# V in 512 columns from four weight blocks held together, in place of two groups of 256

## The chip, the cores and the metric

The kernel runs on one core of one Trainium2 chip, written in Bass with the Tile layer. The metric is the time of one execution on the device in microseconds, as the median of several runs. The core has five engines that work in parallel and in order, each on its own queue: TensorE (PE; its weight loads are listed as PEld), VectorE (DVE), ScalarE (ACT), GpSimd (POOL) and SyncE (SP), which mainly issues DMA transfers. Matmul results go to PSUM, everything else lies in SBUF.

## The reference

One inference step of a streaming encoder layer: a mixer (attention over a band of keys beside a convolution), cross-attention to 256 memory tokens, and a SwiGLU feed-forward. There are 2048 prompt frames and 128 sample frames (8 streams of 16), so 17 tiles of 128 rows, of width 1024. What matters here is the mixer's input projection:

```
h = rmsnorm(x, g_mix_pre)
proj = h @ w_in                      # 1024 -> [q 512 | k 512 | v 512 | u_val 512 | u_gate 512]
q, k, v, u_val, u_gate = jnp.split(proj, ...)
att = band_attention(q, k_ext, v_ext, key_valid, rel_bias)   # 8 heads x 64
u = u_val * jax.nn.sigmoid(u_gate)   # then a depthwise convolution of width 31
```

The keys and values of the last 512 prompt frames and of the sample frames are outputs too.

## The kernel before

**Precision.** Each operand of a matmul is split into a high part (rounded to fp32r) and a low part, the remainder; `mm3` issues three matmuls per product, high by high (L290), high by low (L291) and low by high (L292). A weight block of 128 rows by 1024 words is loaded by SyncE's queue into one of three buffers `wf`, cast by ScalarE into a high buffer `wh` (L283), and the low part `wl` is the difference, by GpSimd in the projection (L285). There are four `wh` and four `wl`, given out in turn; a block can be split only when all matmuls that read the buffer's former block are done.

**The projection** (`phase_proj`) takes the 17 tiles in three groups of 6, 6 and 5 tiles, each in two halves of at most three tiles (384 columns). A group runs, in the order of the code: GLU (four pairs of weight blocks, 384-column matmuls; L605, L606 evict), the V stage, then q and k (eight blocks, `qk`). Transposes of the next group's normed rows (L337, evicted by L339 and L340) lie between. Beside this run the depthwise convolutions of the groups: for three of four channel blocks on VectorE (L523), for the fourth and for the sample rows on ScalarE (L532, the product) and GpSimd (L533, the sum); a call of `tick` draws some of these steps, at V as elsewhere. The product has two buffers, so ScalarE's L532 can be only two steps ahead of GpSimd.

**The V stage.** V is computed with the normed rows as weights and the V weights as the moving operand, so that a tile's rows lie in the partitions. It runs over two groups of 256 columns; for each, two weight blocks (512 input rows each) are loaded, and each tile gets 24 matmuls of 256 columns into the first half of a PSUM buffer. The buffers of 512 words are four (`mm`), given out in turn. ScalarE copies the result into the high half of `vv` (L656), VectorE writes the difference beside it (L657), and SyncE stores both to `vs` in DRAM (L658). `vv` has two buffers. For tiles 12 and later ScalarE also copies the plain values into `vo` (three buffers, L645), which go to the outputs.

**What sets the order.** The kernel is written once in program order; when it is built, a scheduler with a timeline of its own lays down each engine's order from dependences and priorities. Steps of the convolutions that `tick` draws are given a lower priority. So a change in one place can move instructions around it on all engines. `bias_tables` in the first group writes a table for the attention's bias through DRAM, a 2.5 MB transfer on GpSimd's DMA queue (`toep`, L267).

After the projection come the band attention (from about 611 us), the output projection, cross-attention and the feed-forward, the largest part.

Of the kernel before, what the change touches and what calls it, by code (L numbers as in the profile page):

```python
# [8 lines left out]
F32 = mybir.dt.float32  # L9
# [8 lines left out]
P = 128  # L18
D = 1024
KC = D // P  # L20
NPT = 16
S_TILE = 16
H = 8
DH = 64
# [116 lines left out]
class Build:  # L141
# [309 lines left out]
    def phase_proj(self):  # L451
        nc, A = self.nc, self.A
        pool, fa = self.ap, self.fa
        ps_mm = ps_tr = Region().lay(self.ps, 0, ("mm", 2, 4), ("tr", 2, 2), ("ca", 4, 1))
# [43 lines left out]
        def pump(q, n):  # L498
            while n > 0 and q:
                try:  # L500
                    with self.tc.high_priority(offset=-LOWP):
                        next(q[0])
                    n -= 1
                except StopIteration:
                    q.pop(0)
# [4 lines left out]
        def tick():  # L510
            for x, q in enumerate((vq, pq)):
                acc[x] = acc[x] + rates[gi][x] if q else 0.0
                n = int(acc[x])
                pump(q, n)
                acc[x] -= n
# [62 lines left out]
        for gi, subs in enumerate(GROUPS):  # L578
# [5 lines left out]
            hs = nxt  # L584
# [3 lines left out]
            for j in range(4):  # L588
# [6 lines left out]
                wv = self.wload(A["w_in"][12 + j])  # L595
                wg = self.wload(A["w_in"][16 + j])
                off = 0
                for hsub in hs:
                    _, _, n, npc = hsub
# [16 lines left out]
                src = lambda w, u=ut, n=L: u[:, w:w + n]  # L616
# [6 lines left out]
                if npr < len(tiles):  # L623
                    o = ct[:, L:L + P].rearrange("p (s w) -> p s w", w=DEC_S)
                    src = lambda w, j=j: us[:, j, :, w:w + DEC_S]
# [2 lines left out]
                self.bias_tables(Region().lay(fa, 0, ("fb", 3, 1), ("rv", 1, 1)), glu)  # L628
            prev_u = (uts, L)
            x_ = "x" if last else ""  # L630
            for cg in range(2):
                wv = [self.wload(A["w_v"][cg, kh]) for kh in range(2)]
                for hsub, sub in zip(hs, subs):
                    hh, hl, _, _ = hsub
                    for i, t in enumerate(sub):
                        ps = self.t(ps_mm, [P, 512], F32, "mm")
                        tc_ = slice(i * P, (i + 1) * P)
                        for k in range(KC):
                            wh, wl = wv[k // 4]
                            c = slice((k % 4) * 256, (k % 4 + 1) * 256)  # L640
                            self.mm3(ps[:, :256], hh[:, k, tc_], hl[:, k, tc_], wh[:, c], wl[:, c], k == 0, k == KC - 1)
                        tick()
                        if t >= 12:
                            vo = self.t(pool, [P, 256], F32, "vo")
                            nc.scalar.copy(vo[:, :], ps[:, :256])  # L645
                            if t == S_TILE:
                                nc.sync.dma_start(self.vsamp[:, cg * 256:(cg + 1) * 256], vo[:, :])
                                nc.sync.dma_start(
                                    A["new_att_v_new"][:, cg * 256:(cg + 1) * 256], vo[:, :])
                            else:  # L650
                                nc.sync.dma_start(
                                    A["new_att_v_prompt"][(t - 12) * P:(t - 11) * P, cg * 256:(cg + 1) * 256], vo[:, :])
                        if t != S_TILE:
                            vv = self.t(pool, [P, 4, P], F32R, "vv", 2)
                            src = ps[:, :256].rearrange("p (h d) -> p h d", d=DH)
                            nc.scalar.copy(vv[:, :, :DH], src)  # L656
                            nc.vector.tensor_tensor(vv[:, :, DH:], src, vv[:, :, :DH].bitcast(F32), ALU.subtract)  # L657
                            nc.sync.dma_start(self.vs[cg][:, :, t, :], vv[:, :, :].bitcast(F32))  # L658
# [967 lines left out]
def layout(inputs):  # L1626
    import numpy as np

    i = {k: np.asarray(v) for k, v in inputs.items()}
    c = np.ascontiguousarray  # L1630
    o = {}
    o["x_prompt"] = i["x_prompt"].reshape(2048, D)
    o["x_sample"] = i["x_sample"].reshape(P, D)
    o["mem_prompt"] = i["mem_prompt"].reshape(NM, D)
    o["cache_att_k"] = i["cache_att_k"].reshape(DEC_B, PAST, 512)
    o["cache_att_v"] = i["cache_att_v"].reshape(DEC_B, PAST, 512)
    o["cache_conv"] = i["cache_conv"].reshape(DEC_B * HALO, 512)
    o["cache_convT"] = i["cache_conv"].reshape(DEC_B, HALO, 4, P).transpose(3, 2, 0, 1).reshape(P, 4 * DEC_B, HALO)
    o["cache_att_kT"] = i["cache_att_k"].reshape(DEC_B, PAST, 4, P).transpose(0, 3, 2, 1)
    o["cache_mem_kT"] = (i["cache_mem_k"].reshape(DEC_B, NM, 2, 4, P).transpose(0, 2, 4, 3, 1)  # L1640
                         .reshape(DEC_B, 2, P, D))
    o["cache_mem_v"] = i["cache_mem_v"].reshape(DEC_B, NM, D)

    def colblocks(w):
        n = w.shape[1] // P
        return w.reshape(KC, P, n, P).transpose(2, 1, 0, 3).reshape(n, P, D)

    o["w_in"] = colblocks(i["w_in"][0])
    wv = i["w_in"][0][:, 1024:1536]
    o["w_v"] = wv.reshape(2, 4, P, 2, 256).transpose(3, 0, 2, 1, 4).reshape(2, 2, P, D)  # L1650
    o["w_out"] = i["w_out"].reshape(KC, P, D)
    o["w_mk"] = colblocks(i["w_mk"][0])
    o["w_mv"] = colblocks(i["w_mv"][0])
    o["w_mqT"] = i["w_mq"][0].T.reshape(KC, P, D)
    o["w_mq"] = i["w_mq"].reshape(KC, P, D)
    o["w_mo"] = i["w_mo"].reshape(KC, P, D)
    o["w_gate"] = colblocks(i["w_gate"][0])
    o["w_up"] = colblocks(i["w_up"][0])
    o["w_down"] = i["w_down"].reshape(NF, P, D)
    for n in ("g_mix_pre", "g_mix_post", "g_mem_pre", "g_mem_post", "g_mem_kv", "g_ffn_pre", "g_ffn_post"):  # L1660
        o[n] = i[n].reshape(D)
    o["conv_w"] = i["conv_w"][0].reshape(CW, 4, P).transpose(2, 1, 0)
    for n in ("conv_b", "cln_g", "cln_b"):
        o[n] = i[n].reshape(4, P).T
    o["rel_rev"] = i["rel_bias"][0][:, :0:-1]
    return {k: c(v) for k, v in o.items()}
# [38 lines left out]
```

## Time and profile before

| | |
|---|---|
| median of 3 runs | 2940.11 us (2939.65 to 2940.16) |
| the profiled execution | 2931.87 us, its span 2930.0 us, mean granted clock 0.996 |
| TensorE busy | 98% of the span |
| VectorE, ScalarE, GpSimd busy | 73%, 46%, 48% |
| V stages | 178.9 to 216, 358.5 to 393, 525.6 to 554 us |

A row of a timeline has the start in microseconds, the duration, the engine, the line of the kernel, the operation, the tiles (written <- read), the shape, and how many equal instructions it merges; in brackets stands how long the engine was idle before it and whose work ended that. A windows row has the stretch, its length, the busy time (and instructions) of PE, PEld, DVE, ACT and POOL, the granted TensorE clock as a share of full speed, the DMA engines' busy share and GB/s. Matmuls overlap, so their pace is read from start to start.

### The profile page before, as it was taken

The page shows a single profiled execution, that of the slowest core. Times are in us where ns is not written, and L with a number is a line of the kernel's source. Part 1 is how long each engine was busy: PE and PEld are TensorE (multiplying, and loading weights), DVE is VectorE, ACT ScalarE, POOL GpSimd, SP SyncE. Part 2 cuts the span into 40 slices and gives each one's busy share as a digit, 9 for nine tenths or more (in the row PEclk, how much of TensorE's full clock was granted, in tenths as well). Part 3 has the DMA queues.
Part 4 walks back from the last instruction along what each step waited for, and adds up shares of the span by engine and source line. Part 5 has one row for each costly group of instructions (what it writes and reads, how often), then busy time and mean ns, then how long its engine had stood idle before and what let it go on. Part 6 is the DMA issues. An engine that isn't in the chain of part 4 may idle for free.

```text
span 2930.0 us, 45557 instructions
## 1 busy us (share of the span) xinstructions
PE 2878.5 (98%) x16688; PEld 2641.6 (90%) x16688; DVE 2131.4 (73%) x3082; ACT 1339.1 (46%) x2631; POOL 1416.2 (48%) x1334
## 2 busy tenths in 40 slices
PE   9999999989999999999999999999999999999998
PEld 8999999988978887888879999999999999888786
DVE  7687895989985666344559788788888998655656
ACT  4435465678873444232344333433344444333433
POOL 1268495831123443254557555465556775424413
PEclk9999999999999999999999999999999999999999
DMA  8645253665635664233364333544334436756664
GB/s 290 246 135 192 88 164 111 221 225 179 228 132 172 221 223 151 67 127 103 129 199 175 116 134 116 200 156 152 143 137 161 143 143 220 233 171 226 226 217 147
DMA packets 201458, 499.53 MB, mean 170 GB/s; under 512 B 19801, under 2 KB 91361, under 8 KB 192394
## 3 DMA queue, kind: packets, MB, share of 16 engines
q1 hardware_dynamic: 186306, 427.01, 43.2%
q0 software_dynamic: 14928, 69.61, 6.4%
q8 instruction: 131, 2.15, 0.3%
q14 instruction: 93, 0.76, 0.1%
HBM read 365.45 MB, written 141.81 MB: 173 GB/s over the span
## 4 chain that ended last, share of the span: by engine, by line
PE 44%; DVE 3%; DMA 2%; POOL 1%; issue 1%; ACT 0%; SPq 0%; DVEq 0%; POOLq 0%; ACTq 0%
PE psb L292 14%; PE psb L291 14%; PE psb L290 14%; PE psb L298 1%; DMA sbf<-x 1%; PE psb L1373 1%; DMA sbf<-hn 0%; DVE sbr L1588 0%; DMA sbf<-in_w_gate_dram 0%; DVE sbr L1396 0%; DVE sbx L1396 0%; POOL sbf L348 0%; DMA hn<-sbf 0%; DVE flexb L1458 0%; DVE flexb L1460 0%
## 5 line engine op out<-in xcount | busy, mean ns | idle before, releaser
L290 PE MATMUL psb<-sbr 128*128 128x384 f32 (+3 forms) x2808 | 940.3, 336 | 3.9 <-DVE sbx L657 1.5
L291 PE MATMUL psb<-sbr 128*128 128x384 f32 (+3 forms) x2356 | 804.1, 341 | 0.5 <-DVE sbr L340 0.3
L292 PE MATMUL psb<-sbr 128*128 128x512 f32 (+3 forms) x1848 | 633.9, 345 | 4.0 <-DVE sbr L1588 4.0
L290 PEld LDWEIGHTS psb<-sbr 128*128 128x128 f32 x2808 | 529.8, 189 | 33.1 <-DVE sbx L657 1.9
L292 PE MATMUL psb<-sbr,sbx 128*128 128x384 f32 (+2 forms) x1484 | 475.3, 321 | 0.0
L291 PEld LDWEIGHTS psb<-sbr 128*128 128x128 f32 x2356 | 444.2, 189 | 27.6 <-DVE sbr L340 1.0
L292 PEld LDWEIGHTS psb<-sbr 128*128 128x128 f32 x1848 | 348.4, 189 | 33.8 <-DVE sbr L1588 6.8
L298 PE MATMUL psb<-sbr 128*128 128x512 f32 x1200 | 292.7, 393 | 2.4 <-ACT sbr L1266 1.1
L1396 DVE TENSOR_TENSOR sbr<-sbf,sbr 128x512 fp32r<-128x512 f32 x258 | 262.2, 1019 | 39.7 <-ACT sbr L1395 38.5
L1395 ACT CAST sbr<-sbf 128x512 fp32r<-128x512 f32 x258 | 159.2, 620 | 277.9 <-PE psb L291 231.9
L292 PEld LDWEIGHTS psb<-sbr,sbx 128*128 128x128 f32 x1484 | 279.7, 189 | 0.1
L523 DVE SCALAR_TENSOR_TENSOR psb<-sbf,psb 128x768 f32<-128x768 f32 (+1 forms) x290 | 264.3, 912 | 6.2
L298 PEld LDWEIGHTS psb<-sbr 128*128 128x128 f32 x1200 | 222.0, 189 | 48.3 <-POOL sbr L1231 1.3
L1588 DVE TENSOR_TENSOR sbr<-sbf,sbr 128x384 fp32r<-128x384 f32 (+2 forms) x242 | 168.7, 720 | 96.4 <-ACT sbr L1587 95.4
L285 POOL TENSOR_TENSOR sbx<-sbf,sbr 128x1024 fp32r<-128x1024 f32 (+1 forms) x62 | 153.7, 2481 | 80.3 <-ACT sbr L283 69.2
L1587 ACT CAST sbr<-sbf 128x384 fp32r<-128x384 f32 (+2 forms) x242 | 112.6, 483 | 174.4 <-PE psb L291 162.3
L1518 POOL TENSOR_TENSOR sbf<-sbf 128x512 f32<-128x512 f32 x77 | 107.6, 1401 | 165.0 <-DMA sbf<-in_w_down_dram 163.4
L533 POOL TENSOR_TENSOR flexb<-flexb,flexb 128x128 f32<-128x128 f32 (+1 forms) x180 | 168.6, 937 | 26.2 <-ACT flexb L532 17.1
L290 PE MATMUL psb<-sbr,sbx 128*128 128x384 f32 (+1 forms) x524 | 170.6, 327 | 1.3 <-ACT sbr L1375 0.7
L1395 ACT CAST sbx<-sbf 128x512 fp32r<-128x512 f32 x153 | 94.7, 620 | 162.1 <-PE psb L291 149.3
L1396 DVE TENSOR_TENSOR sbx<-sbf,sbx 128x512 fp32r<-128x512 f32 x153 | 154.4, 1011 | 15.1 <-ACT sbx L1395 14.8
L1390 POOL TENSOR_TENSOR sbf<-sbf 128x512 f32<-128x512 f32 x66 | 97.8, 1481 | 108.0 <-DVE sbr L1396 50.8
(330 smaller groups left out, 6084.9 us busy)
## 6 DMA issues: line engine op xcount, KB each, us to landing
af<-flexb SPq DMA_DIRECT2D x33, 1344.0 KB, 5.9
sbf<-in_w_down_dram SPq DMA_DIRECT2D x154, 256.0 KB, 3.6
sbf<-in_w_gate_dram SPq DMA_DIRECT2D x66, 512.0 KB, 3.3
sbf<-in_w_up_dram SPq DMA_DIRECT2D x66, 512.0 KB, 3.4
sbf<-af SPq DMA_DIRECT2D x85, 384.0 KB, 4.1
sbf<-x SPq DMA_DIRECT2D x49, 512.0 KB, 3.7
sbf<-in_w_in_dram SPq DMA_DIRECT2D x48, 512.0 KB, 3.9
sbr<-ks POOLq DMA_DIRECT2D x16, 1024.0 KB, 8.5
```

The costliest lines, as they stand in the source:

```text
L285: self.lo_engine.tensor_tensor(lo[:, c], wf[:, c], hi[:, c].bitcast(F32), ALU.subtract)
L290: nc.tensor.matmul(ps, lh, rh, start=start, stop=False, **kw)
L291: nc.tensor.matmul(ps, lh, rl, start=False, stop=False, **kw)
L292: nc.tensor.matmul(ps, ll, rh, start=False, stop=stop, **kw)
L298: nc.tensor.matmul(y[o], l, r[:, o * 512:(o + 1) * 512], start=start and x == 0, stop=stop and x == 2)
L523: nc.vector.scalar_tensor_tensor(acc if w < CW - 1 else o, src(w), cwt[:, j, w:w + 1], acc, ALU.mult, ALU.add)
L533: nc.gpsimd.tensor_tensor(o, o, v, ALU.add)
L1395: nc.scalar.copy(hs[j][:, :], src[j])
L1396: nc.vector.tensor_tensor(ls[j][:, :], src[j], hs[j][:, :].bitcast(F32), ALU.subtract)
L1518: nc.gpsimd.tensor_tensor(acc[:, :], acc[:, :], q[:, :], ALU.add if s > 0 else ALU.subtract)
L1587: nc.scalar.copy(ch[:, m], a[:, x, m])
L1588: nc.vector.tensor_tensor(cl[:, m], a[:, x, m], ch[:, m].bitcast(F32), ALU.subtract)
```

## The change

The V stage holds four weight blocks of 256 input rows by 512 columns, and runs once over the tiles. A tile gets 24 matmuls of 512 columns into a whole PSUM buffer; the block changes every six matmuls. The two halves of the result are then copied, subtracted and stored one after the other with the same instructions as before, and `tick` is called twice per tile. The layout of the V weights in DRAM follows.

```
-            for cg in range(2):
-                wv = [self.wload(A["w_v"][cg, kh]) for kh in range(2)]
-                for hsub, sub in zip(hs, subs):
...
-                        for k in range(KC):
-                            wh, wl = wv[k // 4]
-                            c = slice((k % 4) * 256, (k % 4 + 1) * 256)
-                            self.mm3(ps[:, :256], hh[:, k, tc_], hl[:, k, tc_], wh[:, c], wl[:, c], k == 0, k == KC - 1)
-                        tick()
...
+            wv = [self.wload(A["w_v"][kq]) for kq in range(4)]
+            for hsub, sub in zip(hs, subs):
+                hh, hl, _, _ = hsub
+                for i, t in enumerate(sub):
+                    ps = self.t(ps_mm, [P, 512], F32, "mm")
+                    tc_ = slice(i * P, (i + 1) * P)
+                    for k in range(KC):
+                        wh, wl = wv[k // 2]
+                        c = slice((k % 2) * 512, (k % 2 + 1) * 512)
+                        self.mm3(ps[:, :], hh[:, k, tc_], hl[:, k, tc_], wh[:, c], wl[:, c], k == 0, k == KC - 1)
+                    tick()
+                    tick()
+                    for cg in range(2) if t >= 12 else ():
+                        cc = slice(cg * 256, (cg + 1) * 256)
+                        vo = self.t(pool, [P, 256], F32, "vo")
+                        nc.scalar.copy(vo[:, :], ps[:, cc])
...
+                    if t != S_TILE:
+                        for cg in range(2):
                             vv = self.t(pool, [P, 4, P], F32R, "vv", 2)
-                            src = ps[:, :256].rearrange("p (h d) -> p h d", d=DH)
+                            src = ps[:, cg * 256:(cg + 1) * 256].rearrange("p (h d) -> p h d", d=DH)
                             nc.scalar.copy(vv[:, :, :DH], src)
                             nc.vector.tensor_tensor(vv[:, :, DH:], src, vv[:, :, :DH].bitcast(F32), ALU.subtract)
                             nc.sync.dma_start(self.vs[cg][:, :, t, :], vv[:, :, :].bitcast(F32))
...
-    o["w_v"] = wv.reshape(2, 4, P, 2, 256).transpose(3, 0, 2, 1, 4).reshape(2, 2, P, D)
+    o["w_v"] = wv.reshape(4, 2, P, 512).transpose(0, 2, 1, 3).reshape(4, P, D)
```

In the changed kernel the plain copies stand in line 646; L656, L657 and L658 keep their numbers.

More of the change, by code (lines that the diff above doesn't have):

```diff
@@ L630, in phase_proj @@
             x_ = "x" if last else ""
-            for cg in range(2):
-                wv = [self.wload(A["w_v"][cg, kh]) for kh in range(2)]
-                for hsub, sub in zip(hs, subs):
[L634 to L637, printed above, removed]
-                        for k in range(KC):
-                            wh, wl = wv[k // 4]
-                            c = slice((k % 4) * 256, (k % 4 + 1) * 256)
-                            self.mm3(ps[:, :256], hh[:, k, tc_], hl[:, k, tc_], wh[:, c], wl[:, c], k == 0, k == KC - 1)
-                        tick()
[L643 to L653, printed above, removed]
@@ new lines, in phase_proj @@
+            wv = [self.wload(A["w_v"][kq]) for kq in range(4)]
[14 more added lines that the diff above has]
+                        nc.scalar.copy(vo[:, :], ps[:, cc])
+                        if t == S_TILE:
+                            nc.sync.dma_start(self.vsamp[:, cc], vo[:, :])
+                            nc.sync.dma_start(A["new_att_v_new"][:, cc], vo[:, :])
+                        else:
+                            nc.sync.dma_start(A["new_att_v_prompt"][(t - 12) * P:(t - 11) * P, cc], vo[:, :])
+                    if t != S_TILE:
+                        for cg in range(2):
```

## Prediction

> **What bounds the kernel now.** I read the page's busy times first, then the windows view over the stage that the change touches (179 to 554 us, in three parts), then TensorE's timeline for its pace and its gaps, then the timelines of ScalarE and GpSimd for what feeds it.
>
> ```profile
> span 2930.0 us, 45557 instructions
> PE 2878.5 (98%) x16688; PEld 2641.6 (90%) x16688; DVE 2131.4 (73%) x3082; ACT 1339.1 (46%) x2631; POOL 1416.2 (48%) x1334
> ```
>
> TensorE is busy for 98% of the span. Windows of the three V stages and of the entry to the attention (columns: window; its length; busy time and instructions of PE, PEld, DVE, ACT, POOL; granted clock; DMA share; GB/s):
>
> ```profile
> 179.00:199.00 20.00, 20.00 (x169) 20.00 (x168) 16.71 (x20) 9.94 (x13) 17.67 (x10) 1.00 0.56 190
> 199.00:216.00 17.00, 15.51 (x128) 15.07 (x127) 12.90 (x18) 8.61 (x16) 11.75 (x7) 1.00 0.61 197
> 358.00:393.00 35.00, 35.00 (x293) 35.00 (x292) 31.37 (x40) 21.07 (x30) 31.57 (x18) 1.00 0.45 137
> 525.00:554.00 29.00, 29.00 (x244) 29.00 (x243) 26.39 (x40) 20.93 (x54) 23.18 (x34) 1.00 0.72 226
> 610.00:640.00 30.00, 22.46 (x125) 17.80 (x124) 22.24 (x60) 22.27 (x59) 8.15 (x16) 0.83 0.54 195
> ```
>
> In the V stages TensorE leaves 1.5 us idle in the first and nothing in the others. So whatever the change takes from TensorE's work there is won in full, and whatever wait it puts before TensorE is lost in full.
>
> **The matmuls.** The change turns 816 matmuls of 256 columns (17 tiles x 2 column groups x 8 x 3) into 408 of 512. TensorE's timeline gives both paces, start to start:
>
> ```profile
> 178.93 0.28 PE L290 MATMUL psb<-sbr 128*128 128x256 f32 x1
> ...
> 358.45 0.28 PE L290 MATMUL psb<-sbr 128*128 128x256 f32 x1
> ...
> 392.87 0.28 PE L292 MATMUL psb<-sbr 128*128 128x256 f32 x1
> ...
> 554.37 0.34 PE L290 MATMUL psb<-sbr 128*128 128x384 f32 x1
> ...
> 2599.69 0.39 PE L290 MATMUL psb<-sbr 128*128 128x512 f32 x1
> ...
> 2605.81 0.39 PE L290 MATMUL psb<-sbr 128*128 128x512 f32 x1
> ```
>
> The second and third are the 1st and 288th matmul of the second V stage: 34.42/287 = 0.120 us. The last two are 27 steps apart in the last phase: 6.12/27 = 0.2267 us. The first row begins the first V stage; the one at 554.37 follows the third, which thus began 240 x 0.120 earlier, at 525.6. Two of 256 cost 0.240, one of 512 costs 0.227; the difference of 0.0132 us, 408 times, is **-5.4 us** (-1.9, -1.9, -1.6 by stage). The stages shrink to 144 x 0.2267 = 32.6, 32.6 and, with five tiles, 27.2 us. The Trainium skill (TensorE: Matmul & The Clock Gate, in the part on 56 against 53.3 ns) puts the fixed cost of a warm matmul at about 2.5 ns beyond its columns; by that 408 matmuls fewer would save only 1.0 us and the sum below would be 4.4 us higher. Here the rows show some 13 ns of it, and I go by the rows.
>
> The two gaps of the first stage come from V copies that were late to free a PSUM buffer:
>
> ```profile
> 200.46 0.39 PE L290 MATMUL psb<-sbr 128*128 128x256 f32 x1 [0.78 <-DVE sbx L657]
> 204.30 0.39 PE L290 MATMUL psb<-sbr 128*128 128x256 f32 x1 [0.70 <-DVE sbx L657]
> ```
>
> A V tile now fills one whole buffer in place of two halves, so four buffers hold 21.8 us of V work and not 11.5; these waits go: **-1.5 us**. What is late next in that place is below.
>
> **The start of a stage.** Weights are split by ScalarE (L283) and then GpSimd (L285) into a ring of four high and four low buffers. A stage used four V blocks before and uses four now; only when each is needed changes. Before, the blocks of the second group were due 17 us in; now all four are due in the first tile.
>
> ```profile
> 179.00 1.05 ACT L283 CAST sbr<-sbf 128x1024 fp32r<-128x1024 f32 x1 [2.72 <-POOL sbx L285]
> ...
> 180.13 2.58 POOL L285 TENSOR_TENSOR sbx<-sbf,sbr 128x1024 fp32r<-128x1024 f32 x1 [1.76 <-ACT sbr L283]
> ```
>
> This is the last V block of the first stage, ready at 182.7, 3.8 us after the stage began (178.9). The order of the built program covers it: TensorE runs the first two blocks' matmuls of tiles one and two (24 x 0.227 = 5.4 us) first, and in the third stage 44 matmuls. I cost the start at nothing; without that cover it would be 1 us a stage. By the same order the first tile ends with the stage's 46th matmul, 10.4 us in (third stage: 55th, 12.5 us).
>
> **The end of a stage.** This decides. The first K block that follows V takes the first buffer of the ring. Before, that was free halfway through V, and its split was long done:
>
> ```profile
> 375.61 2.42 POOL L285 TENSOR_TENSOR sbx<-sbf,sbr 128x1024 fp32r<-128x1024 f32 x1
> ```
>
> That is K's first block in the second stage, ready at 378.0, 15 us before V's last matmul. Now the buffer is held until six matmuls into the last V tile, 18 x 0.227 = 4.1 us before the end; cast and subtraction take 1.05 + 2.4 = 3.5 us. It would just do if ScalarE and GpSimd were at hand. But in ScalarE's order of the built program the cast stands behind the ninth of twelve V copies, and behind conv steps that wait for GpSimd (first stage):
>
> ```
> 113 L656 TensorCopy sbx<-psb 128x4x64 [waits DMAHW2,PE,Activation]
> 114 L532 Activation flexb<-sbf 128x768 [waits Pool]
> 115 L283 TensorCopy sbr<-sbf 128x1024 [waits PE]
> ```
>
> In GpSimd's, K's subtraction stands behind 14 conv adds of the stage. And a V copy needs one of two `vv` buffers, whose last store has to have landed. So the ninth copy comes no sooner than the first one plus four turns of that ring (copy, VectorE's subtraction, store). Before, it stood behind the third (at 195.36, below).
>
> *First stage.* Its stores share the DMA engines with a large table transfer:
>
> ```profile
> 184.94 1.32 POOL L267 DMA_DIRECT2D toep<-fd  x1 [0.24 <-issue]
> ...
> toep<-fd POOLq DMA_DIRECT2D x1, 2560.0 KB, 18.0
> ```
>
> ```profile
> 189.34 0.37 ACT L656 CAST sbx<-psb 128x256 fp32r<-128x256 f32 x1 [3.42 <-DMA vs<-sbx]
> ...
> 195.36 1.04 ACT L283 CAST sbr<-sbf 128x1024 fp32r<-128x1024 f32 x1
> ...
> 199.58 0.37 ACT L656 CAST sbx<-psb 128x256 fp32r<-128x256 f32 x1 [3.18 <-DMA vs<-sbx]
> 199.85 0.94 ACT L532 ACTIVATE flexb<-sbf 128x768 f32<-128x768 f32 x1
> ...
> 203.41 0.37 ACT L656 CAST sbx<-psb 128x256 fp32r<-128x256 f32 x1 [1.69 <-DMA vs<-sbx]
> ...
> 208.11 0.37 ACT L656 CAST sbx<-psb 128x256 fp32r<-128x256 f32 x1 [2.74 <-DMA vs<-sbx]
> ...
> 211.85 0.37 ACT L656 CAST sbx<-psb 128x256 fp32r<-128x256 f32 x1 [1.43 <-DMA vs<-sbx]
> ```
>
> ```profile
> 189.75 0.42 DVE L657 TENSOR_TENSOR sbx<-psb,sbx 128x256 fp32r<-128x256 f32 x1 [1.21 <-ACT sbx L656]
> ...
> 200.93 1.85 POOL L533 TENSOR_TENSOR flexb<-flexb,flexb 128x768 f32<-128x768 f32 x1 [0.25 <-ACT flexb L532]
> ```
>
> ```profile
> ACT sbx L656 <- DMA vs<-sbx: 14.4, 7, 3.4
> ```
>
> ```profile
> DMA to landing us min/median/max: 2.5/3.7/14.8
> ```
>
> (The last two fences: ScalarE's waits from 179 to 222 us, in sum, times, longest; and the V stores' time to landing, over all of them.) The table lands near 203, and the store for which the copy at 203.41 waited, that of the data subtracted at 189.75, took 13 us. The copies at 203.41, 208.11 and 211.85 are the fifth, seventh and ninth: turns of 4.7 and 3.7; I take 4.5, since the copy of a tile's second half now also waits for VectorE's subtraction of the first. After the change the first pair is copied at 189.5 and 191.5, its stores run in the same shadow, and the third copy comes at 201.5 to 203.3. Three turns on, the ninth is at 215.0 to 216.8. A conv step (0.9) and the cast (1.05) end at 217 to 219; GpSimd does its 14th add (1.85) after that conv step, then K's subtraction (2.4): ready at 220.4 to 222.2. TensorE ends V at 178.9 + 32.6 = 211.5, has 0.8 us of transposes and, by its order, 1.0 us of matmuls that need no low half. Stall: 7.1 to 8.9, I take **+8 us**. Bounds: 0 (stores land in 3 us; then the cast meets the 3.5 us that it has) and 12 (turns of 5.5).
>
> *Second stage.* No table. A turn is copy 0.37, subtraction 0.42 and the median 3.7 of a store, 4.5. First copy 10.7 us in, ninth at 28.7 (just after TensorE frees the buffer), cast 30.5; GpSimd's 14 adds of 1.85 and a gap or two also end near 30.5; low half 32.9. TensorE needs it at 32.6 + 0.8 + 1.0 = 34.4: **0**, covered by 1.5 us. A turn of 5.5 would use that up and cost 2.
>
> *Third stage.* Here K's cast stands behind the seventh copy, a prompt copy (L645, after L646) goes with each V copy, and VectorE reaches the first subtraction only after L558 and eleven conv steps (from 532.1, 0.74 each and a little between), near 541.
>
> ```profile
> 530.69 1.47 DVE L558 SCALAR_TENSOR_TENSOR flexb<-flexb 128x512 f32<-128x512 f32 x1
> 532.08 0.74 DVE L523 SCALAR_TENSOR_TENSOR psb<-sbf,psb 128x512 f32<-128x512 f32 x1
> ```
>
> ```profile
> 539.49 0.37 ACT L656 CAST sbx<-psb 128x256 fp32r<-128x256 f32 x1 [0.89 <-DMA vs<-sbx]
> 540.87 1.05 ACT L283 CAST sbr<-sbf 128x1024 fp32r<-128x1024 f32 x1
> ...
> 544.23 0.38 ACT L656 CAST sbx<-psb 128x256 fp32r<-128x256 f32 x1 [0.22 <-DMA vs<-sbx]
> ```
>
> Before, K's cast came at 540.87, 13 us ahead of need, and a turn was 544.23 - 539.49 = 4.7. After: first copy 538.5, its store from 541 lands near 545; third copy 545, fifth 549.7, seventh 554.4; conv step and cast 556.4, subtraction 558.8. TensorE ends V at 525.6 + 27.2 = 552.8, with 0.4 of transposes and 0.6 of matmuls in hand: 553.8. Stall **+5 us**; bounds 0 and 8.
>
> **The clock.** A stall of this length costs more than itself. Elsewhere in this trace:
>
> ```profile
> 1122.76 1.76 PE L325 MATMUL psb<-ident,sbf 128*128 128x128 f32 x7 [3.23 <-DVE sbr L327]
> ```
>
> ```profile
> 1122.00:1124.00 2.00, 1.24 (x6) 1.25 (x7) 2.00 (x2) 0.00 (x0) 2.00 (x2) 0.64 0.58 223
> 1124.00:1126.00 2.00, 2.00 (x8) 1.71 (x7) 2.00 (x3) 1.24 (x2) 1.84 (x3) 0.50 0.59 221
> 1126.00:1128.00 2.00, 2.00 (x11) 1.63 (x10) 2.00 (x3) 0.72 (x1) 0.49 (x1) 1.00 0.98 299
> ```
>
> After 3.2 us of idleness the clock is at half for 2 x 0.72 + 2.0 = 3.4 us; busy TensorE loses 1.7 of it. Two stalls: **+3.4 us**; bounds 0 and 7 (two such stretches each). The Trainium skill (the same page, Part 1) says that an idle window of about 3.4 us halves the clock until a busy one has passed; the trace agrees, with half clock in the rows above.
>
> **What costs nothing.** Twelve V weight loads of 512 KB remain twelve, in the same places of SyncE's queue but for their contents; V copies, subtractions and stores are as many and as large as before; two steps of the conv work are drawn per tile where one was drawn per half tile. The cover is that TensorE does not wait for them, except as costed. At the attention's entry TensorE idles 7.5 of 30 us (610 to 640) behind VectorE's leftovers; VectorE may get ahead during the third stall and give some of it back: 0, bound -4.
>
> **The sum.** -5.4 - 1.5 + 8 + 0 + 5 + 3.4 = +9.5 us. The profiled execution took 2931.87 us (span 2930.0); it becomes 2941.4. The median of the runs, 2940.11, stands 8.2 higher; I carry that over: 2949.6.
>
> **Rivals.**
> - *The ring keeps up* (ends faster). If a turn is 4 us or less in all stages, K is split in time, no clock dip comes, and -6.9 us is left: 2933.2. For it: the second stage, and stores of under 3 us where little else runs. Against it: the seven waits of the first stage, 14.4 us in sum, above. It decides at a ninth copy 29.6 us into the first stage (the cast and the subtraction then end at 34.4).
> - *One stall only.* The third stage is covered, say because VectorE reaches the first subtraction sooner: 2949.6 - 5 - 1.7 = 2942.9, which is within the measurement. The first stall stays, since the table transfer stays.
> - *Longer turns.* At 5.5 us the first stall is 12, the third 7, the second 2 with its own dip: 2949.6 + 4 + 2 + 2 + 1.7 = 2959.3. For it: the subtraction of each first half now stands between two copies.
>
> **Numbers.** The forecast 0.60, longer turns 0.10, one stall 0.22, the ring keeps up 0.08. Differences under 0.2% (5.9 us) I count as no change: slower 0.70, same 0.22, faster 0.08. The range, 2936 to 2961, leaves out most of the faster case and what is beyond the longer turns; the forecast's own range is 2944 to 2957.
>
> **What would show it.** TensorE's 512-column V matmuls 0.227 apart. In the first stage a gap of 5 to 11 us near 212, ended by ScalarE's L283 or GpSimd's L285, with the ninth copy waiting for a store; no such gap in the second; one of 3 to 7 near 553 (moved by what came before). A granted clock of 0.5 behind each. It is wrong if the stores of the first stage's first pair land in 4 us, if the ring turns in under 4, or if the attention's entry, whose order of work also changes, moves by more than 4 us.

## The result

The changed kernel takes 2944.9 us (median of 22 runs, 2941.4 to 2949.2), the kernel before 2939.2 us beside it (22 runs): ratio 1.0017, 95% interval [1.0011, 1.0024], or +5.7 us. In a second set of runs the same code was at 1.0034 [1.0021, 1.0047]. Both intervals lie above 1, so it is slower. But 5.7 us is a little under the 5.9 us (0.2%) below which I had said I would count no change; the second set is above it. The forecast was 2949.6 us, and slower; the reasons held only in part.

The profiled execution has a span of 2941.4 us (before: 2930.0). Of these 11.4 us, 0.8 lie ahead of the first V stage and 2.7 behind the attention, where the order of instructions is the same in both kernels. I measure that last part, from the output projection's first matmul to the end, at 2082 to 2092 us over fourteen profiles, whatever the kernel. A difference of spans thus says little here, and below I compare stretches.

The page of the changed kernel:

```profile
span 2941.4 us, 44724 instructions
PE 2877.8 (98%) x16280; PEld 2619.7 (89%) x16280; DVE 2135.5 (73%) x3082; ACT 1339.0 (46%) x2631; POOL 1416.7 (48%) x1334
```

TensorE's windows around the end of the three V stages and at the attention's entry (window; length; busy time and instructions; granted clock; DMA share; GB/s), before:

```profile
210.00:230.00 20.00, 20.00 (x137) 1.00 0.70 215
310.00:400.00 90.00, 90.00 (x628) 1.00 0.36 112
525.00:560.00 35.00, 35.00 (x284) 1.00 0.69 217
615.00:660.00 45.00, 38.41 (x259) 0.89 0.67 243
```

and after:

```profile
210.00:230.00 20.00, 15.13 (x73) 0.83 0.61 190
310.00:400.00 90.00, 90.00 (x497) 1.00 0.29 95
525.00:560.00 35.00, 34.02 (x171) 1.00 0.50 160
615.00:660.00 45.00, 31.13 (x205) 0.89 0.61 207
```

The first line is the stall that I forecast: 4.9 us idle, and the clock. The second has none, as forecast. The third loses 1.0 us where I had 5. The last, the entry, loses 7.3 us more than before, and the forecast has nothing there. TensorE's rows of the two stalls, and the first and the last of the 144 matmuls of the second stage:

```profile
215.70 0.44 PE L290 MATMUL psb<-sbr 128*128 128x384 f32 x1 [2.21 <-ACT sbr L283]
216.92 0.44 PE L290 MATMUL psb<-sbr 128*128 128x384 f32 x1 [0.25 <-ACT sbr L283]
219.94 0.69 PE L292 MATMUL psb<-sbr,sbx 128*128 128x384 f32 x1 [2.41 <-POOL sbx L285]
...
363.42 0.39 PE L290 MATMUL psb<-sbr 128*128 128x512 f32 x1
...
395.88 0.40 PE L292 MATMUL psb<-sbr 128*128 128x512 f32 x1
...
558.05 0.44 PE L292 MATMUL psb<-sbr,sbx 128*128 128x384 f32 x1 [0.97 <-POOL sbx L285]
```

32.46/143 = 0.2270 us for a matmul of 512 columns. The first stage's stall is made as forecast. ScalarE's V copies (the third, fifth, seventh and ninth) wait for a store, and K's cast stands behind the ninth:

```profile
202.77 0.37 ACT L656 CAST sbx<-psb 128x256 fp32r<-128x256 f32 x1 [7.03 <-DMA vs<-sbx]
...
206.27 0.37 ACT L656 CAST sbx<-psb 128x256 fp32r<-128x256 f32 x1 [1.16 <-DMA vs<-sbx]
...
209.85 0.38 ACT L656 CAST sbx<-psb 128x256 fp32r<-128x256 f32 x1 [0.92 <-DMA vs<-sbx]
...
213.43 0.37 ACT L656 CAST sbx<-psb 128x256 fp32r<-128x256 f32 x1 [0.63 <-DMA vs<-sbx]
214.62 1.03 ACT L283 CAST sbr<-sbf 128x1024 fp32r<-128x1024 f32 x1
```

GpSimd, which has to subtract for K, waits too, for the conv product that stands behind ScalarE's waiting copy. It then has seven adds to do, and comes to K only at 217.5:

```profile
204.16 13.41 POOL L533 TENSOR_TENSOR flexb<-flexb,flexb 128x768 f32<-128x768 f32 x7 [5.54 <-ACT flexb L532]
217.53 4.70 POOL L285 TENSOR_TENSOR sbx<-sbf,sbr 128x1024 fp32r<-128x1024 f32 x2
```

At the entry the timeline shows one new gap of TensorE, and ScalarE's wait behind it (rows of ScalarE, SyncE's queue, GpSimd and TensorE, after):

```profile
626.93 1.51 ACT L554 ACTIVATE sbf<-psb,sbf 128x128 f32<-128x128 f32 x4 [1.44 <-DMA cs<-sbf]
...
644.66 1.50 ACT L554 ACTIVATE sbf<-psb,sbf 128x128 f32<-128x128 f32 x4 [5.15 <-DMA cs<-sbf]
...
624.85 1.71 SPq L559 DMA_DIRECT2D cs<-sbf  x2
631.23 2.61 SPq L559 DMA_DIRECT2D cs<-sbf  x2
...
629.20 0.64 POOL L815 DMA_DIRECT2D sbr<-qs  x1
...
646.22 0.90 PE L853 MATMUL psb<-ident,flexb 128*128 128x128 f32 x3 [5.49 <-ACT sbf L554]
```

and the same place before:

```profile
628.16 0.33 SPq L559 DMA_DIRECT2D cs<-sbf  x1
632.97 0.33 SPq L559 DMA_DIRECT2D cs<-sbf  x1
...
629.13 0.64 POOL L815 DMA_DIRECT2D sbr<-qs  x1
...
632.36 1.51 ACT L554 ACTIVATE sbf<-psb,sbf 128x128 f32<-128x128 f32 x4 [0.59 <-PE psb L551]
```

Here the convolution's last norms (`conv_norm`) run among the attention's first steps. Each writes its tile into one of two buffers (L554), which a store then empties (L559). At 629 us GpSimd's queue starts the load of the second head, four transfers of 1 MB. Before, the third tile's store left at 628.16, ahead of that load, and the fifth tile found its buffer free. After, the order of instructions is another: the first two tiles are done together, the third waits for the first store, and its own store leaves at 631.23, behind the load (and behind one of 512 KB on SyncE's own queue, last section). The fifth tile waits for it until 644.66, and the transposes of the attention (L853) stand behind.

### The profile page after: what moved, and what is told of

Read it like the earlier page. It is cut to its first block, busy times and chain, and to the rows that moved or that the text cites. A ratio compares the mean times of both kernels' runs of the same rounds, so it can differ in the third digit from the quotient of the medians.

```text
span 2941.4 us, 44724 instructions
## 1 busy us (share of the span) xinstructions
PE 2877.8 (98%) x16280; PEld 2619.7 (89%) x16280; DVE 2135.5 (73%) x3082; ACT 1339.0 (46%) x2631; POOL 1416.7 (48%) x1334
## 4 chain that ended last, share of the span: by engine, by line
PE 41%; DMA 4%; DVE 3%; POOL 3%; issue 2%; ACT 0%; SPq 0%; DVEq 0%; POOLq 0%; ACTq 0%
PE psb L292 13%; PE psb L290 13%; PE psb L291 13%; DMA sbf<-in_w_down_dram 2%; POOL sbf L1518 1%; PE psb L298 1%; DMA sbf<-x 1%; PE psb L1373 1%; DMA sbf<-hn 0%; DVE sbr L1588 0%; DVE sbr L1396 0%; POOL sbf L348 0%; DMA hn<-sbf 0%; DVE sbr L1522 0%; DVE flexb L1458 0%
## 5 line engine op out<-in xcount | busy, mean ns | idle before, releaser
L290 PE MATMUL psb<-sbr 128*128 128x384 f32 (+3 forms) x2672 | 916.2, 345 | 7.4 <-ACT sbr L283 2.5
L291 PE MATMUL psb<-sbr 128*128 128x384 f32 (+3 forms) x2356 | 804.5, 342 | 0.7 <-DVE sbr L340 0.3
L292 PE MATMUL psb<-sbr 128*128 128x512 f32 (+2 forms) x1712 | 609.2, 358 | 3.7 <-DVE sbr L1588 3.5
L290 PEld LDWEIGHTS psb<-sbr 128*128 128x128 f32 x2672 | 503.4, 189 | 43.0 <-ACT sbr L1587 4.1
L291 PEld LDWEIGHTS psb<-sbr 128*128 128x128 f32 x2356 | 444.8, 189 | 27.6 <-DVE sbr L340 1.0
L292 PEld LDWEIGHTS psb<-sbr 128*128 128x128 f32 x1712 | 321.5, 188 | 39.8 <-DVE sbr L1588 7.7
L298 PEld LDWEIGHTS psb<-sbr 128*128 128x128 f32 x1200 | 222.5, 189 | 48.9 <-ACT sbr L1266 1.3
L1518 POOL TENSOR_TENSOR sbf<-sbf 128x512 f32<-128x512 f32 x77 | 106.9, 1393 | 168.7 <-DMA sbf<-in_w_down_dram 167.0
L283 ACT CAST sbr<-sbf 128x1024 fp32r<-128x1024 f32 x98 | 102.4, 1050 | 111.4 <-PE psb L291 58.9
```

Source lines behind the costliest of these rows:

```text
L290: nc.tensor.matmul(ps, lh, rh, start=start, stop=False, **kw)
L291: nc.tensor.matmul(ps, lh, rl, start=False, stop=False, **kw)
L292: nc.tensor.matmul(ps, ll, rh, start=False, stop=stop, **kw)
L298: nc.tensor.matmul(y[o], l, r[:, o * 512:(o + 1) * 512], start=start and x == 0, stop=stop and x == 2)
L1518: nc.gpsimd.tensor_tensor(acc[:, :], acc[:, :], q[:, :], ALU.add if s > 0 else ALU.subtract)
```

## Experiments

Each kernel's time is set against the runs of the kernel before on the same chip. The change's own rows are its first set. The stretches are from each kernel's own profile: stage 1 from its first V matmul to the first transposes of the conv norm (L538); stages 2 and 3 from the second stage's first V matmul to the first scores (L836); entry from there to the first matmul of the output projection. Between the first two lie 51.1 us in every profile.

| kernel | stage 1 | stages 2, 3 | entry | ratio to before, 95% | us |
|---|---|---|---|---|---|
| before | 128.4 | 252.9 | 236.3 | | |
| the change | 132.5 | 250.8 | 242.1 | 1.0017 [1.0011, 1.0024] | +5.7 |
| after_again | 133.0 | 253.1 | 243.7 | 1.0034 [1.0021, 1.0047] | +11.4 |
| groups_0_1 | 132.9 | 251.0 | 236.6 | 0.9998 [0.9989, 1.0006] | -0.5 |
| group_2 | 128.8 | 254.5 | 242.9 | 1.0018 [1.0010, 1.0027] | +5.7 |
| group_1 | 128.4 | 252.3 | 234.7 | 0.9981 [0.9972, 0.9990] | -5.2 |
| four_z | 132.7 | 253.9 | 229.2 | 0.9976 [0.9967, 0.9984] | -8.8 |
| toep_later | 128.2 | 250.8 | 243.3 | 1.0009 [0.9999, 1.0019] | +1.9 |
| three_vv | 133.2 | 251.0 | 241.6 | 1.0016 [1.0007, 1.0025] | +4.0 |
| all_three | 128.9 | 251.3 | 228.2 | 0.9953 [0.9939, 0.9966] | -16.1 |
| before_four_z | 128.8 | 252.9 | 234.0 | 0.9993 [0.9984, 1.0002] | -2.8 |
| before_four_z_toep | 127.0 | 252.9 | 234.7 | 0.9988 [0.9979, 0.9996] | -3.6 |
| change_four_z_toep | 128.8 | 251.2 | 228.0 | 0.9970 [0.9960, 0.9981] | -9.3 |
| all_three_again | 127.5 | 252.4 | 230.9 | 0.9968 [0.9956, 0.9981] | -7.7 |

(us: difference of the medians.)

### Where the loss is: the change by groups

Theory A: most of the loss is the entry's wait, a consequence of the new order in the third group. Theory B: it is stage 1's stall, and the entry's gap an accident of one execution.

> The changed kernel once more, for a second profile of it. Shown by the first: a stall of 2.21 + 0.25 + 2.41 = 4.9 us ahead of the first K block of stage 1 with 6.8 us at half clock behind it, 0.97 us in stage 3, and one gap of 5.49 us at the attention's entry (646.2 us), where ACT waits 5.15 us for the store of a finished tile. If these belong to the change, all three come back within about 1 us each, and the times lie about 5.7 us over before. If the profile of one execution is what differed, the entry's gap or the stall of stage 1 is missing or moved, and the span is nearer to before's than 11.4 us.

The three waits came back, all of them, but the time did not: +11.4 us where 5.7 were expected. The stall is 2.60 + 2.39 us in stage 1, 1.01 in stage 3, and at the entry

```profile
652.13 0.90 PE L853 MATMUL psb<-ident,flexb 128*128 128x128 f32 x3 [5.62 <-ACT sbf L554]
```

Three kernels then give each group its own form, with both layouts of the V weights in DRAM (here the first; `group_2` and `group_1` have `(2,)` and `(1,)`):

```
+            if gi in (0, 1):
                 wv = [self.wload(A["w_v"][kq]) for kq in range(4)]
...
+            else:
+                for cg in range(2):
+                    wv = [self.wload(A["w_v2"][cg, kh]) for kh in range(2)]
...
```

> 512 columns at a time in the first two groups, the old two column groups in the third (which restores the old order of work at the attention's entry). Theory A, that the entry pays most of the loss: only stage 1's stall is left, so +5.0 - 0.8 (there already before the edit) - 1.9 (stage 2's faster matmuls) = about +2.3 us against before, no gap over 2 us on TensorE between 640 and 650 us. Theory B, that the stall of stage 1 pays it: +4 to +6 us, as much as the whole change.

> 512 columns at a time in the third group alone. Theory A: stage 3 gains 1.6 us (27.2 us of matmuls with 0.97 us of stall behind them), the entry with its new order loses about 5.8, so +4 us against before, and the gap of about 5 us that ends with the store of a finished tile is in the profile. Theory B: the gap of the entry is an accident of one execution, and the kernel is 1 to 2 us faster than before.

> 512 columns at a time in the second group alone, where neither profile shows a stall. Both theories: 144 matmuls of 0.227 us in place of 288 of 0.120 us, 1.9 us faster than before, no new gap. If it is not faster, the gain of the longer matmuls is taken back later (at the entry, by the head's load or the clock).

The third group alone pays +5.7 us: as much as the whole change in its first set, half of it in the set run beside these kernels (+11.4). Its entry has the gap (6.16 us), its stage 1 is as before. With the first two groups the entry is at 236.6 and stage 1 pays 4.5 us, but the time is level with before (theory A's +2.3 lies just outside the interval, -3.2 to +1.8). So the entry's loss belongs to the third group's edit and is no accident: theory A for the place. Stage 1's loss is real too, about 5 us between `groups_0_1` and `group_1`; the second group about pays for it there. The parts (-0.5 and +5.7) add up to the first set of the whole change, but not to the second; the stretches of its second profile are 4.4 us longer in sum than those of its first, and why I can't show. The second group alone gave 5.2 us where 1.9 were expected, and 1.9 lie outside its interval (2.9 to 8.2). Its matmuls show the 1.9 us (32.85 against 34.70 us for the stage); where the other 3 come from I can't show.

What decides at the entry is on which side of the load the third store leaves. `group_1`, with the old order:

```profile
631.53 0.33 SPq L559 DMA_DIRECT2D cs<-sbf  x1
...
632.50 0.64 POOL L845 DMA_DIRECT2D sbr<-qs  x1
```

`group_2`, with the new one:

```profile
633.35 0.34 SPq L559 DMA_DIRECT2D cs<-sbf  x1
...
631.11 0.64 POOL L845 DMA_DIRECT2D sbr<-qs  x1
```

With two buffers, the third store leaves 1.0 us before the load in the three profiles with the old order, and 2.0 to 2.2 us after it in the five with the new. ScalarE's wait of 4.6 to 5.8 us is in those five and in none of the three.

### The entry's remedy: more buffers

```
-                   .lay(sbF, 2, ("thx", 2, 1), ("zx", 2, 2), ("xnx", 2, 2))
+                   .lay(sbF, 2, ("thx", 2, 1)).at("zx", 2, (sbF, [4, 6, 22, 24])).lay(sbF, 8, ("xnx", 2, 2))
```

> The changed kernel with four buffers for the finished tile of the late norms where there were two; nothing else is edited. Theory A (the entry's loss is ACT's wait for a tile's store that stands behind the second head's load): both waits of ACT for that store (1.4 and 5.2 us) and the gap of 5.5 us on TensorE go, and the stretch from the first scores to the first matmul of the output projection falls from 242 - 244 to 236 - 238 us, 5 to 6 us less in all: level with before. Rival D (the load itself holds up whatever comes next, so the wait only changes its name): the stretch stays over 241 us, and the gap ends with the load of the head or of a sample.

Both waits are gone; the fifth tile (the second row) comes 18.8 us after the first scores (618.95), where it came 30.5 us after them (614.19) in the change (timeline of ScalarE, and SyncE's queue):

```profile
631.11 2.88 ACT L554 ACTIVATE sbf<-psb,sbf 128x128 f32<-128x128 f32 x8
637.79 1.51 ACT L554 ACTIVATE sbf<-psb,sbf 128x128 f32<-128x128 f32 x4 [0.17 <-PE psb L551]
...
636.45 2.25 SPq L559 DMA_DIRECT2D cs<-sbf  x2
```

Theory A's mechanism is shown, and rival D fails: no other wait takes the place. The gain is larger than forecast: the entry's stretch falls by 13 us, to 7 less than before the change. TensorE's idle time in the stretch is 8.3 us less (18.1 to 9.8). Little of the rest is the clock. With the gap, TensorE idles for more than half of 640 to 650 us, with the clock at half for much of it (the change):

```profile
640.00:650.00 10.00, 4.21 (x18) 0.57 0.50 176
```

and with four buffers not:

```profile
640.00:650.00 10.00, 8.88 (x79) 1.00 1.04 384
```

But half clock costs only where TensorE works. In the change that is 5.2 us of the stretch (641.5 to 651.7), a loss of 2.6; and `four_z` has a half-clock stretch of its own (622.9 to 626.3), in which TensorE works throughout and loses 1.7:

```profile
624.00:626.00 2.00, 2.00 (x10) 0.50 0.07 19
```

So the clock gives about 1 us; where the other 4 come from I can't show.

### Stage 1's remedies: the table later, a third buffer

```
-        nc.gpsimd.dma_start(toep[:, :, :], bass.AP(f0.tensor, f0.offset + 127, [[768, H], [-1, P], [1, 5 * P]]))
...
+        return lambda: nc.gpsimd.dma_start(
+            toep[:, :, :], bass.AP(f0.tensor, f0.offset + 127, [[768, H], [-1, P], [1, 5 * P]]))
...
                 wv = self.wload(A["w_in"][12 + j])
+                if gi == 1 and j == 0:
+                    with self.tc.issue_after(self.last_lo.ins):
+                        spread()
```

> The changed kernel with the transfer of the bias table (16.7 us long) moved out of the V stage of the first group, behind the split of the first weight block of the second group. Theory S (the stores of V tiles of stage 1 stand in the shadow of that transfer, and ACT with them): ACT's wait of 7.0 us for a store and the stall of 4.9 to 5.6 us ahead of K go down to under 1 us, as in stage 2, and with them the 6.8 us of half clock; 5 to 7 us less than the change as it is. Rival R (the four weight blocks held together, or the ring of two alone, make K's split late): the stall stays at 3 us or more.

Without the table beside it the stage has no stall; copies wait 1.2 us at most, and the clock stays up. Later in the stretch TensorE waits once for a normed tile, and the clock then stands at 0.50 from 292.4 to 295.8, so that 4.3 us of the stretch are won and not the whole of stall and clock:

```profile
210.00:230.00 20.00, 20.00 (x116) 1.00 0.69 232
```

```profile
290.96 1.09 PE L338 MATMUL psb<-ident,sbf 128*128 128x128 f32 x8 [1.86 <-DVE sbf L334]
```

Theory S holds for the place and the cause; in the time it is 3.8 us less than the change's first set, short of the 5 to 7 expected (9.5 less than its second). The stretch, 4.3 us, is the firmer figure.

```
-                   .lay(sbR, 104, ("vv", 2, 2)))
+                   .at("vv", 2, (sbR, [104, 106]), (fa, [25])))
```

> The changed kernel with three buffers for the split V tile in place of two. Theory S: the wait behind the table's transfer is shared by three buffers, so that the last copies come about a third earlier: stall of stage 1 from 4.9 - 5.6 to 1 - 3 us, the 0.97 us of stage 3 to none, 3 to 5 us less than the change as it is. Rival R (the weight buffers are what K waits for): both stalls as before within 0.5 us.

A miss: the stall was 3.60 + 2.00 us in stage 1, and 0.63 in stage 3. The third buffer moves the long wait one copy on, from 202.77 [7.03] to

```profile
205.66 0.37 ACT L656 CAST sbx<-psb 128x256 fp32r<-128x256 f32 x1 [8.51 <-DMA vs<-sbx]
```

since a store waits for the end of the table's transfer whatever the count, and then GpSimd has again its seven adds ahead of K. So the count of these buffers isn't what stage 1 lacks; nor do the four weight blocks alone make the stall (rival R), or `toep_later` would have kept it.

### What the change is worth without its side effects

These kernels combine the edits shown above: `all_three` and its repeat have the four buffers, the later table and the third `vv` buffer; the others what their names say, on the V stage before or that of the change.

> The change with all three of these edits: four buffers for the finished tile, three for the split V tile, the table's transfer later. If the loss is stage 1's stall with its clock and the entry's wait, and nothing else, what is left is the gain of the matmuls: 408 x (2 x 0.120 - 0.227) = 5.4 us, and the kernel is 4 to 7 us faster than before. If the causes only change their names, it is within 2 us of before.

> The kernel before (two column groups of 256) with the four buffers for the finished tile. It has no wait for such a store to lose. Theory A alone: the stretch from the first scores to the first matmul of the output projection stays at 236 us, time within 2 us of before. If the four buffers also take away the half clock of the entry (10.2 us in every kernel with two buffers, none in the one with four), the stretch falls to about 230 us here too, 5 to 7 us faster than before, and that much of the gain of the changed kernel with four buffers is not the change's.

> The kernel before with the four buffers and with the table's transfer later, the base for the change with both causes of its loss removed. If the transfer also makes the two gaps of 0.7 to 1.2 us between V's matmuls in stage 1 of the kernel before, those go, 1.5 us less than with the four buffers alone; if not, level with it.

> The change with the four buffers and the later transfer, two buffers for the split V tile as in the change itself. Against the kernel before with the same two edits only the V stages differ: 5.4 us for the matmuls less 1.0 us of stage 3's stall = 4 to 5 us faster than that kernel. If the change is worth nothing by itself, the two are level within 2 us.

> The change with all three edits once more, for its interval and beside the one without the third buffer of the split V tile: 13 us faster than before as it was, and 0 to 1 us faster than with two buffers (stage 3's stall).

With the same two edits in both kernels, the change takes 2931.7 us and the kernel before 2937.4, run side by side: 5.7 us less, a little over the 4 to 5 expected (their intervals against before, -11.8 to -5.6 and -6.2 to -1.2 us, leave room for much more or nearly none). The size is met, the place is not: in the two profiles the V stages come out level. Stage 1 has 1.9 us less of matmuls (32.84 against 34.71) but is 1.8 longer, with a wait of 2.46 us for a normed tile; stages 2 and 3 give 1.7; 6.7 come at the entry, where in these profiles the clock fell in one and not in the other: TensorE works for 12.2 us at half clock in the first and not at all in the second, 6.1 us (630 to 640 us, first `before_four_z_toep`, then `change_four_z_toep`):

```profile
630.00:640.00 10.00, 8.42 (x43) 0.72 0.91 335
```

```profile
630.00:640.00 10.00, 8.31 (x58) 1.00 0.91 331
```

That is not firm. In `all_three_again`, whose code is that of `all_three`, the clock fell:

```profile
630.00:640.00 10.00, 8.71 (x48) 0.73 1.01 366
```

and its entry is 2.7 us longer. `before_four_z` has such a stretch too and is level with before within its interval: the four buffers alone are not the gain, and they do not take the half clock away. (Over the entry's stretch it is 6.8 to 13.7 us in the eight profiles with two buffers, and 3.4 in `four_z`: neither the 10.2 nor the none that I had put down.) `before_four_z_toep` lost both PSUM gaps in stage 1, 1.5 us, so these were also the table's. The two sets of `all_three` differ (-16.1 us where 4 to 7 less were expected, then -7.7 where 13 were); their intervals meet near 0.996. The third `vv` buffer shows no gain beside the other two edits. All versions of the change with four buffers are faster than both kernels, by 0.2 to 0.5% of the kernel before.

## Why the prediction was right or wrong

- **The matmuls, -5.4.** Right: 0.2270 us where I took 0.2267, the second stage 1.84 us shorter, the third 27.2 us long. By the fixed cost that the Trainium skill states (TensorE: Matmul & The Clock Gate, in the part on 56 against 53.3 ns) the second stage would have gained, as an estimate, 0.4 us; the trace does not agree.
- **The PSUM waits, -1.5, and the start of a stage, 0.** Right.
- **Stage 1's stall, +8 (0 to 12).** Mechanism right, the term was too large: 4.9 and 5.0 us. The third copy came at 202.77 (I had 201.5 to 203.3); a turn of the ring was 3.5 us, not 4.5, and the ninth copy was at 213.43. I had worked a turn out with a store of 3.7 us (the second stage), and there I misread a view. That median is over every transfer of `vs`, and the attention's eight loads of 1 MB are among them. The view by issues has the 32 V stores alone, before and after:

```profile
vs<-sbx SPq DMA_DIRECT2D x32, 256.0 KB, 2.9
...
vs<-sbx SPq DMA_DIRECT2D x32, 256.0 KB, 2.6
```

With 2.9 in place of 3.7 the same sum gives a turn of 3.7. The last part of the stall was GpSimd's backlog: the cast had ended at 215.65, and its seven adds held K's subtraction until 217.53.

- **Stage 2, 0.** Right.
- **Stage 3's stall, +5 (0 to 8).** Too large: 1.0 us, by the same turn (543.16 to 553.91 for three: 3.6).
- **The clock, +3.4.** One stretch, not two, but twice as long: by the rows below, and 0.50 between them, half clock from 218.2 to 225.0. TensorE worked for the last 5.1 of it, a loss of 2.5 us. The 1 us of stage 3 caused none; in `toep_later` a single wait of 1.86 us was followed by half clock for 3.4, in `all_three_again` one of 2.01 us, at the same place, by none.

```profile
218.00:220.00 2.00, 0.06 (x1) 0.55 1.03 323
...
224.00:226.00 2.00, 2.00 (x10) 0.74 0.95 335
```

- **The entry, 0, bound -4.** This step failed. I saw that its order would change, named it as what would make me wrong, and yet bounded it to one side only. It cost 5.8 and 7.4 us in the two profiles, as much as the whole change in its first set. A row that I had could have told of it: a ring of two whose store left 1.0 us ahead of a 4 MB load.
- **The sum.** In the stretches of the first profile: -5.4 - 1.5 + 4.9 + 1.0 + 2.5 + 5.8 = +7.3; measured from the first V matmul to the output projection +7.8. The forecast's +9.5 came near it by luck: stalls and clock were 8 us too high in sum and the entry 6 too low. The 8.2 us that I carried from the profiled execution to the median was 1.7 for the changed kernel (2943.2 against 2944.9): a difference between two single executions, and no property of the kernel.
- **The rivals.** "The ring keeps up" had the turn right (3.5 us), but its point of decision, a ninth copy 29.6 us into the stage, was missed by 4 us, as the table alone delayed the third by 7. "One stall only" was nearest in the stages: the third was covered but for 1 us, though for its shorter turns and not for an earlier VectorE (its first V copy came at 543.16, 1.6 us later than forecast after the shift of the stage's start). "Longer turns" was wrong.
- **The signs.** Two of the three signs named for being wrong came: the ring turned in under 4 us, and the entry moved by more than 4. Of the others, the gap of stage 1 was just under the 5 to 11 named; that of stage 3 was 1.0 where 3 to 7 were named, without half clock behind it.

## What to carry to other kernels

When an edit makes a stage hold its buffers to the end, follow what the next stage's first load must pass on every engine's queue, and ask what bulk transfer delays the items in it. Where a built order changes near a ring of two buffers that are emptied by stores, price a loss as well as a gain: a store that leaves a microsecond or two after a bulk load rather than before it can cost the length of the load, above all when its own queue moves in small packets and the load in large ones (next section). And compare stretches of a profile, not spans, where identical code varies by more than the edit is worth.

## What was unexpected of the hardware

The third tile's store has 256 KB. Such a store lands in 2.0 us when little else runs (the first tile's); behind the load, the third's, issued at 631.23, held the fifth tile until 644.66, 13.4 us later. In the view of the `cs` transfers of the changed kernel's entry the longest, 11.7 us, is the fourth tile's, issued at 633.5; the third's landing is not told:

```profile
DMA to landing us min/median/max: 2.0/2.0/11.7
```

From 630 to 640 us the DMA engines moved 366 GB/s:

```profile
630.00:640.00 10.00, 7.05 (x44) 1.00 1.00 366
```

Ahead of the third store on its own queue was one load of 512 KB:

```profile
630.04 0.57 SPq L758 DMA_DIRECT2D sbf<-in_cache_att_kT_dram  x1
```

The Trainium skill (DMA: Bandwidth & Descriptors, in the part on the queue model, "Arbitration") says that each engine takes turns between its queues, packet by packet. If equal turns meant equal bytes, the store and that load would need, as an estimate, 0.77 MB at half of 366 GB/s, 4.2 us, and 2 to land: less than half of what it took. The trace agrees with the rule all the same, for the turns are equal in packets and not in bytes. These are the packets, the MB and the share of the engines' time from 634 to 642 us, for GpSimd's queue (q0) and SyncE's (q1):

```profile
q0 software_dynamic: 383, 2.88, 91.5%
q1 hardware_dynamic: 370, 0.38, 17.0%
```

A packet of GpSimd's loads has 7.5 KB on average, one of the 512 KB load 1.0 KB. So SyncE's queue moved an eighth of the other's bytes, and the store's turn came only when that load was through. Stage 1 shows the same: from 194 to 200 us of the kernel before, the table's queue and that of the V stores moved 222 packets each, 1.14 and 0.11 MB. In the old order the third store left ahead of both loads; no run here tells which of the two alone would have held it up.
